# Reloading the residual on GpSimd's queue, and tying the first casts of a wide weight stage in order

## The chip, the cores and the metric

The kernel runs on one core of a Trainium2 chip. Its time is the device time of one execution in microseconds. The kernel before took 2210.05 us, the median of 3 runs (2208.66 to 2213.14).

The engines of the core are named as the profile names them: PE (TensorE, matrix products; PEld is its weight load), DVE (VectorE), ACT (ScalarE), POOL (GpSimd) and SP (SyncE). Each takes its own instructions strictly in order. SP does no arithmetic here: its list is a list of DMAs, and where one of them has to wait for a semaphore, all that stand behind it wait too. POOL can issue DMAs as well.

## The reference

One layer of a transformer-like encoder on 256 tokens of width 2048, all in float32: a SwiGLU feed-forward block (FFN1), a mixer of attention and a linear recurrence, a cross-attention, and a second feed-forward block (FFN2). The change touches only the second half of the two feed-forward blocks: the product with `w_down` (5504 x 2048) and what follows it.

```python
def rmsnorm(x, g, eps=EPS):
    xf = x.astype(jnp.float32)
    y = xf * lax.rsqrt(jnp.mean(xf * xf, axis=-1, keepdims=True) + eps)
    return (y * g.astype(jnp.float32)).astype(x.dtype)

def swiglu(h, w_gate, w_up, w_down):
    return (jax.nn.silu(h @ w_gate) * (h @ w_up)) @ w_down
...
h = rmsnorm(x, n_ffn1_pre[l])
x = x + 0.5 * rmsnorm(swiglu(h, w_ffn1_gate[l], w_ffn1_up[l], w_ffn1_down[l]), n_ffn1_post[l])
```

FFN2 is the same with its own weights. The `x` that is added at the end is the residual: in FFN1 the kernel's input (`in_x` in the profile), in FFN2 a copy in HBM (`xsp`).

## The kernel before

**Numbers in two parts.** A float32 product is made of three products in a faster format (float32r). Each weight tile that a DMA brings (`raw`, 128 x 1024, 512 KB) is cast on ACT to a high part (`hi`), and DVE subtracts that from the raw tile to get the low part (`lo`). PE then does high x high, high x low and low x high. So each tile needs one cast on ACT and one split on DVE before PE can use it, and its raw buffer comes free when the split is done.

**The down projection.** `ffn` first makes the hidden activations (`mh`, `ml`, 43 blocks k of 128 rows). Then `lin` runs over c = 0 to 3, the four groups of 512 output columns, two groups (b = 0: c 0 and 1, b = 1: c 2 and 3) at a time:

- For even c, the **wide part** (`lin_wide`) takes k = 0 to 29 with tiles of 1024 columns, which serve both groups. Its order is 0, 1, 2, the pair (4, 5), 3, 18, the pair (6, 7), 19, 20 and so on to the pair (16, 17) and 29. A single k costs PE 12 products: 2 token halves x 2 column halves x 3. A pair is multiplied in a Strassen-like way: its two raw tiles, here called ra and rb, are cut four times, w11 (the first half of ra), then rb as it is (w21 and w22), then, after four additions on DVE that overwrite them (L566 to L569), ra again (e1 and e3) and rb again (e4 and e2). PE uses them in the order w11, w21, w22, e1, e3, e2, e4, three products each, 21 in all. `cut` (L527) issues the cast and the split; the six slots of hi and lo that they fill go round: three are `whi`/`wlo` slots, which the other products use as well, and three are called `room`. The sums of activations that pairs need stand in `S`; those of the first five pairs lie in the buffer with the tag `big`.
- Then a **narrow part** takes k = 30 to 42 with tiles of 512 columns, two k per tile: first k = 30 to 35 of the odd group (`narrow(c + 1, ...)`), then 30 to 42 of the even one, and, in the next call of `lin`, the rest of the odd one. That is 36 + 78 + 42 = 156 products of 512 columns on PE for each b. The work of `fix_wide`, which adds the shared sums of the wide part to the results, stands between them on DVE.

**Loads.** Weight tiles go round four buffers `wraw`, and in the wide part also the two halves of `raws` (the 5th and 6th of each six loads). All are issued from SP, so a load waits on SP until the split that frees its buffer is done, and what stands behind it waits as well.

**The residual X.** `X` takes the buffer `big` again, so it can be loaded when the first five pairs of b = 1 are done. `refill` (L875) issues its four pieces (two token halves t, two column halves, 512 KB each) in the narrow part of c = 2 from SP's queue, each tied with `after` behind the last split that was written before it. `refill(k)` is called for k = 30, 33, 36 and 39, and the loop that calls it passes each k twice (once for each t): eight loads. The second of each two writes the same bytes as the first, and waits for it.

**What sets the order.** PE's order is written out by hand in these parts. On ACT, DVE, SP and POOL a scheduler places instructions by priority (`ahead` raises it) and by its own estimate of when they are ready; ties made by `after` bind it. The fixed order on each engine is the result.

Of the kernel before, what the change touches and what calls it, by code (L numbers as in the profile page):

```python
# [10 lines left out]
F32 = mybir.dt.float32  # L11
# [7 lines left out]
P = 128  # L19
D = 2048  # L20
T = 256
NT = T // P
# [14 lines left out]
SPAIRS = range(2, 9)  # L37
WIDE, EARLY = 30, 36


def _wide_order():

    rest = [k for k in range(WIDE) if k // 2 not in SPAIRS]
    out, rest = rest[:3], rest[3:]
    for i in SPAIRS:
        out.append((2 * i, 2 * i + 1))
        out, rest = out + rest[:2], rest[2:]
    assert not rest
    return out
# [176 lines left out]
class Layer:  # L226
# [288 lines left out]
        self.split(d[:, 0], mh[:, k, P:], ml[:, k, P:])  # L515
        self.split(d[:, 1:], sh, sl)

    def lin_wide(self, w, b, mh, ml, sums, ring, raws, banks):

        nc = self.nc
        own, shared = banks
        seen, turn = set(), [0]
        last = _wide_order()[-1]

        def cut(raw):  # L527
            n = raw.shape[-1]
            hi, lo = (x[:, :n] for x in ring[turn[0] % len(ring)])
            turn[0] += 1  # L530
            with self.ahead(self.lead):
                self.last_cast = nc.scalar.copy(out=hi, in_=raw)  # L532
                self.last_split = nc.vector.tensor_sub(out=lo, in0=raw, in1=hi.bitcast(F32))  # L533
            return [(self.paired(hi[:, i : i + 512]), self.paired(lo[:, i : i + 512])) for i in range(0, n, 512)]

        def product(bank, x, wt, stop=False):
            (xh, xl), (hi, lo) = x, wt
            start = id(bank) not in seen
            seen.add(id(bank))
            nc.tensor.matmul(bank, xh, hi, start=start, stop=False)  # L540
            nc.tensor.matmul(bank, xh, lo, start=False, stop=False)  # L541
            nc.tensor.matmul(bank, xl, hi, start=False, stop=stop)  # L542

        def load():
            i = self.wide_at % 6
            raw = raws[:, i - 4] if i > 3 else self.wraw.tile([P, WT], F32, tag="wraw", name="wraw")
            o = P * WT * (b * KF + self.wide_at)
            nc.sync.dma_start(out=raw, in_=w[o : o + P * WT].rearrange("(p x) -> p x", p=P))
            self.wide_at += 1
            return raw  # L550

        at = lambda k, t: tuple(x[:, k, t * P : (t + 1) * P] for x in (mh, ml))
        self.wide_at = 0
        for item in _wide_order():
            if isinstance(item, int):
                halves = cut(load())
                for t in range(NT):
                    for h in range(2):
                        product(own[t][h], at(item, t), halves[h], item == last)
                continue  # L560
            k0, k1 = item
            ra, rb = load(), load()
            a0, a1, b0, b1 = ra[:, :512], ra[:, 512:], rb[:, :512], rb[:, 512:]
            (w11,), (w21, w22) = cut(a0), cut(rb)
            with self.ahead(self.lead):
                nc.vector.tensor_add(a0, a0, a1)  # L566
                nc.vector.tensor_add(a1, a1, b1)  # L567
                nc.vector.tensor_add(b1, a0, b1)
                nc.vector.tensor_add(b0, b1, b0)  # L569
            (e1, e3), (e4, e2) = cut(ra), cut(rb)  # L570
            s2, s3, s4 = sums(k0 // 2 - SPAIRS[0])
            end = k0 // 2 == SPAIRS[-1]
            product(shared[0], at(k0, 0), w11, end)
            product(own[0][0], at(k1, 0), w21)
            product(own[0][1], s4, w22)
            product(shared[1], at(k0, 1), e1, end)
            product(shared[2], s3, e3, end)
            product(shared[3], s2, e2, end)
            product(own[1][0], at(k1, 1), e4)
        self.cuts = turn[0]  # L580

    def fix_wide(self, banks, part):
# [210 lines left out]
    def ffn(self, normed, wg, wu, wd, post, residual, *after):  # L793
        nc = self.nc
        passage = normed if isinstance(normed, Passage) else None
        h, row, *feed = (passage.h, passage.row) if passage else normed
        with self.tc.tile_pool(name="hid", bufs=1) as hid:
            mh = hid.tile([P, KF, T], F32R, tag="mh", name="mh")
            ml = hid.tile([P, KF, T], F32R, tag="ml", name="ml")
# [3 lines left out]
            def sums(n):  # L803
                x, n = (S[0], n) if n < 5 else (S[1], n - 5)
                return x[:, 3 * n : 3 * n + 3]
# [24 lines left out]
            for c0 in range(0, DFF, 256):  # L830
                n = min(256, DFF - c0)
# [38 lines left out]
            raws = self.hpool.tile([P, 2, WT], F32, tag="hT", name="raws", bufs=4)  # L870
            slots = [(self.whi[:, a : a + WT], self.wlo[:, a : a + WT]) for a in range(0, RING * SLOT, SLOT)]
            more = [(x[:, 0], x[:, 1]) for x in room]
            fresh = {}

            def refill(k):  # L875
                i = (k - WIDE) // 3
                if "X" in fresh and i < 4:
                    t, s = i // 2, slice(i % 2 * 1024, (i % 2 + 1) * 1024)
                    self.after(nc.sync.dma_start(
                        out=fresh["X"][:, t, s], in_=residual[t * P : (t + 1) * P, s]), self.last_split)  # L880

            banks = {}

            def narrow(c, ks, ev, *args):
                base = c // 2 * KF * P * WT + (WIDE * WT + c % 2 * (KF - WIDE) * 512) * P
                for k in self.lin_tok_steps(
                        wd, KF, 0, 512, mh, ml, ev, *args, 0, [banks[c // 2][0][t][c % 2] for t in range(NT)],
                        (ks, lambda k: base + (k - WIDE) * P * 512)):
                    if c == 2 and k % 3 == WIDE % 3:
                        refill(k)  # L890

            def lin(c, ev, passage):
                b = c // 2
                if c % 2:
                    narrow(c, range(EARLY, KF, 2), ev, (7 if passage else SKEW) * (c == 3), passage)
                    return
                make = lambda pool, tag: [pool.tile([P, 512], F32, tag=tag, name="mm") for _ in range(2)]
                one = [make(self.pst, "tr"), make(self.pss, "sm")]
                two = [make(self.psm, "mm"), make(self.psm, "mm")]
                own, shared = (two, one) if b else (one, two)  # L900
                banks[b] = [list(x) for x in zip(*own)], [x for p in shared for x in p]
                with self.tc.manual_schedule(engines={mybir.EngineType.PE}):
                    order = slots[self.turn :] + slots[: self.turn]
                    self.lin_wide(wd, b, mh, ml, lambda n: [(x[:, 0], x[:, 1]) for x in (sums(n)[:, i] for i in range(3))],
                                  order + more, raws, banks[b])
                    self.turn = (self.turn + self.cuts % (2 * RING)) % RING if self.cuts % (2 * RING) < RING else self.turn
                    narrow(c + 1, range(WIDE, EARLY, 2), None, 0, None)
                    self.fix_wide(banks[b], self.wraw.tile([P, WT], F32, tag="wraw", name="part"))
                    if b:
                        self.X = fresh["X"] = self.hpool.tile([P, NT, D], F32, tag="big", bufs=1, name="X")  # L910
                    narrow(c, range(WIDE, KF, 2), ev, 0, None)

            return self.post_norm(lin, post, True, *after)

    def rope_tables(self, tp):
# [1022 lines left out]
```

## Time and profile before

| | |
|---|---|
| median of 3 runs | 2210.05 us |
| the profiled execution | 2216.57 us |
| span of its trace | 2214.7 us |
| granted PE clock over the span | 0.996 |
| FFN1, wide part of b = 0 / narrow / wide part of b = 1 / narrow | begins at 460.8 / 537.9 / 571.5 / 644.7 us |
| FFN2, the same | begins at 1980.0 / 2053.6 / 2087.3 / 2160.4 us |
| DMAs X<-in_x and X<-xsp in the two narrow parts | 8 and 8, 512 KB each |

Times in the trace count from the span's start. "Busy" of PE is the modelled duration of its pipelined products, which overlap: how far PE is from its pace is read from the starts and the number of its products. A row of the timeline gives the start, the duration, the engine, the line, the operation with its output and inputs, and in brackets the idle time of the engine before it with what ended that. A wait in the list of waits is followed by the total in us, the number of times and the longest.

### The profile page before, as it was taken

The page shows a single profiled execution, that of the slowest core. Times are in us where ns is not written, and L with a number is a line of the kernel's source. Part 1 is how long each engine was busy: PE and PEld are TensorE (multiplying, and loading weights), DVE is VectorE, ACT ScalarE, POOL GpSimd, SP SyncE. Part 2 cuts the span into 40 slices and gives each one's busy share as a digit, 9 for nine tenths or more (in the row PEclk, how much of TensorE's full clock was granted, in tenths as well). Part 3 has the DMA queues.
Part 4 walks back from the last instruction along what each step waited for, and adds up shares of the span by engine and source line. Part 5 has one row for each costly group of instructions (what it writes and reads, how often), then busy time and mean ns, then how long its engine had stood idle before and what let it go on. Part 6 is the DMA issues. An engine that isn't in the chain of part 4 may idle for free.

```text
span 2214.7 us, 35352 instructions
## 1 busy us (share of the span) xinstructions
PE 2170.6 (98%) x13580; PEld 1929.0 (87%) x13580; DVE 1618.7 (73%) x2402; ACT 1189.7 (54%) x1794; POOL 106.0 (5%) x177
## 2 busy tenths in 40 slices
PE   9999999999998999999999999999999999999997
PEld 8999999988887888988777889988999999988885
DVE  7777666688876677777787767657777766679795
ACT  7555555555545665664444556446555555555452
POOL 0000000000000100101342000000000000000000
PEclk9999999999999999999999999999999999999999
DMA  7666666665757664555867765546666666666755
GB/s 248 201 199 203 202 202 201 200 228 196 227 196 260 201 224 142 187 176 181 250 196 241 269 219 191 177 165 219 200 199 202 201 201 202 202 215 220 222 200 199
DMA packets 133512, 457.70 MB, mean 207 GB/s; under 512 B 16480, under 2 KB 18016, under 8 KB 133088
## 3 DMA queue, kind: packets, MB, share of 16 engines
q1 hardware_dynamic: 125712, 438.23, 60.4%
q0 software_dynamic: 6768, 16.79, 2.5%
q8 instruction: 106, 1.74, 0.3%
q10 hardware_dynamic: 864, 0.44, 0.1%
q14 instruction: 62, 0.51, 0.1%
HBM read 442.80 MB, written 12.59 MB: 206 GB/s over the span
## 4 chain that ended last, share of the span: by engine, by line
PE 80%; issue 7%; DMA 4%; DVE 4%; ACT 2%; POOL 1%; SPq 0%; DVEq 0%; POOLq 0%; ACTq 0%
PE mm L421 31%; PE mm L425 15%; PE mm L460 6%; PE mm L461 6%; PE mm L462 6%; PE mm L541 4%; PE mm L542 4%; PE mm L540 4%; DVE wlo L366 2%; ACT whi L365 1%; DMA wraw<-in_w_ffn_down 1%; DMA raws<-in_w_ffn_down 1%; DMA X<-xsp 0%; DMA X<-in_x 0%; DMA ab<-vsh 0%
## 5 line engine op out<-in xcount | busy, mean ns | idle before, releaser
L366 DVE TENSOR_TENSOR wlo<-wraw,whi 128x1024 fp32r<-128x1024 f32 (+3 forms) x672 | 806.4, 1203 | 434.9 <-ACT whi L365 426.4
L421 PE MATMUL mm<-hT,whi 128*128 128x512 f32 x3280 | 1078.2, 384 | 2.6 <-ACT whi L365 2.0
L365 ACT CAST whi<-wraw 128x1024 fp32r<-128x1024 f32 (+3 forms) x672 | 691.4, 1031 | 594.9 <-PE mm L462 209.0
L425 PE MATMUL mm<-hT,wlo 128*128 128x256 f32 x3280 | 879.7, 273 | 0.0
L421 PEld LDWEIGHTS mm<-hT,whi 128*128 128x128 f32 x3280 | 614.1, 190 | 83.7 <-ACT whi L365 3.2
L425 PEld LDWEIGHTS mm<-hT,wlo 128*128 128x128 f32 x3280 | 629.6, 192 | 6.1 <-DVE wlo L366 0.5
L461 PE MATMUL mm<-wlo,hT 128*128 128x512 f32 (+2 forms) x512 | 180.3, 352 | 3.7 <-DVE wlo L366 3.5
L460 PE MATMUL mm<-whi,hT 128*128 128x512 f32 (+2 forms) x512 | 182.5, 356 | 0.9 <-DVE gt L1597 0.7
L462 PE MATMUL mm<-whi,hT 128*128 128x512 f32 (+2 forms) x512 | 178.3, 349 | 0.3 <-DVE hT L649 0.3
L433 ACT COPY half<-mm 128x256 f32<-128x256 f32 x206 | 75.7, 368 | 115.7 <-PE mm L421 115.7
L434 DVE TENSOR_TENSOR half<-half,mm 128x256 f32<-128x256 f32 x206 | 85.9, 418 | 40.3 <-ACT half L433 40.3
L461 PEld LDWEIGHTS mm<-wlo,hT 128*128 128x128 f32 x512 | 97.1, 190 | 18.7 <-DVE wlo L366 10.1
L541 PE MATMUL mm<-wlo,mh 128*128 128x512 f32 x284 | 108.4, 382 | 1.1 <-DVE wlo L533 1.0
L540 PE MATMUL mm<-whi,mh 128*128 128x512 f32 x284 | 108.5, 382 | 0.7 <-ACT whi L532 0.7
L542 PE MATMUL mm<-whi,ml 128*128 128x512 f32 x284 | 108.4, 382 | 0.0
L460 PEld LDWEIGHTS mm<-whi,hT 128*128 128x128 f32 x512 | 97.1, 190 | 12.5 <-DVE gt L1597 1.1
L462 PEld LDWEIGHTS mm<-whi,hT 128*128 128x128 f32 x512 | 97.1, 190 | 9.9 <-DVE hT L649 1.2
L613 POOL TENSOR_TENSOR rstd<-rstd,mhalf 128x1 f32<-128x1 f32 x22 | 15.3, 704 | 1707.5 <-DVE rstd L611 1707.5
L461 PE MATMUL mm<-wlo,mh 128*128 128x512 f32 x200 | 78.2, 391 | 6.5 <-DVE wlo L366 6.5
L532 ACT CAST room<-wraw 128x1024 fp32r<-128x1024 f32 (+1 forms) x56 | 49.7, 893 | 63.3 <-DVE wraw L567 53.2
L460 PE MATMUL mm<-whi,mh 128*128 128x512 f32 x200 | 77.5, 388 | 5.1 <-ACT whi L365 5.1
L533 DVE TENSOR_TENSOR wlo<-wraw,whi 128x1024 fp32r<-128x1024 f32 x60 | 71.8, 1222 | 14.5 <-ACT whi L532 13.7
(371 smaller groups left out, 2834.6 us busy)
## 6 DMA issues: line engine op xcount, KB each, us to landing
wraw<-in_w_ffn_up SPq DMA_DIRECT2D x171, 512.0 KB, 4.2
wraw<-in_w_ffn_gate SPq DMA_DIRECT2D x170, 512.0 KB, 4.3
wraw<-in_w_ffn_down SPq DMA_DIRECT2D x128, 512.0 KB, 4.8
wraw<-in_w_in SPq DMA_DIRECT2D x124, 512.0 KB, 4.1
raws<-in_w_ffn_down SPq DMA_DIRECT2D x40, 512.0 KB, 4.8
wraw<-in_w_o SPq DMA_DIRECT2D x32, 512.0 KB, 4.2
wraw<-in_w_ckv SPq DMA_DIRECT2D x32, 512.0 KB, 3.5
wraw<-in_w_oa SPq DMA_DIRECT2D x16, 512.0 KB, 3.5
```

Of the source, the lines that this page charges most:

```text
L365: cast = self.last_cast = nc.scalar.copy(out=hi[:, e], in_=raw[:, e])
L366: self.last_split = nc.vector.tensor_sub(out=lo[:, e], in0=raw[:, e], in1=hi[:, e].bitcast(F32))
L421: both = lambda: nc.tensor.matmul(ps[j], hi[:, s], self.woven(x[:, k]), start=(k == 0), stop=(k == nk - 1))
L425: nc.tensor.matmul(ps[j][:, 0, :], lo[:, s], self.woven(x[:, k, 0]), start=False, stop=False)
L433: nc.scalar.copy(out=tokens, in_=low)
L434: nc.vector.tensor_add(tokens, tokens, high)
L460: nc.tensor.matmul(ps[t], part(xh, t, k), hi, start=(k == first and not begun), stop=False, **more)
L461: nc.tensor.matmul(ps[t], part(xh, t, k), lo, start=False, stop=False, **more)
L462: self.last_mm = nc.tensor.matmul(ps[t], part(xl, t, k), hi, start=False, stop=(k == last), **more)
L540: nc.tensor.matmul(bank, xh, hi, start=start, stop=False)
L541: nc.tensor.matmul(bank, xh, lo, start=False, stop=False)
L542: nc.tensor.matmul(bank, xl, hi, start=False, stop=stop)
```

## The change

It does two things.

**X moves.** The four loads of X are issued from POOL's queue and no longer from SP's, and once each: they are popped from a list. X's tile is made before the wide part of b = 1. `lin_wide` calls `done` behind each pair; behind the last two pairs, (14, 15) and (16, 17), that issues pieces 0 and 1. Pieces 2 and 3 are issued in the narrow part at k = 30. Each is tied behind the last split written before it.

**Ties.** In each wide part the first five calls of `cut` (those of k = 0, 1, 2, w11 and the first rb) are tied: cast behind the cast before it, split behind the split before it.

```diff
@@ lin_wide @@
+            before = self.last_cast, self.last_split
             with self.ahead(self.lead):
                 self.last_cast = nc.scalar.copy(out=hi, in_=raw)
                 self.last_split = nc.vector.tensor_sub(out=lo, in0=raw, in1=hi.bitcast(F32))
+            if turn[0] < 6:
+                for ins, prev in zip((self.last_cast, self.last_split), before):
+                    self.after(ins, prev)
...
             product(own[1][0], at(k1, 1), e4)
+            done(k0 // 2 - SPAIRS[0])
@@ ffn @@
-            fresh = {}
-
-            def refill(k):
-                i = (k - WIDE) // 3
-                if "X" in fresh and i < 4:
-                    t, s = i // 2, slice(i % 2 * 1024, (i % 2 + 1) * 1024)
-                    self.after(nc.sync.dma_start(
-                        out=fresh["X"][:, t, s], in_=residual[t * P : (t + 1) * P, s]), self.last_split)
+            fresh = []
+
+            def refill():
+                i = fresh.pop()
+                t, s = i // 2, slice(i % 2 * 1024, (i % 2 + 1) * 1024)
+                self.after(nc.gpsimd.dma_start(
+                    out=self.X[:, t, s], in_=residual[t * P : (t + 1) * P, s]), self.last_split)
...
-                    if c == 2 and k % 3 == WIDE % 3:
-                        refill(k)
+                    if fresh and k % 5 == WIDE % 5:
+                        refill()
...
+                    if b:
+                        self.X = self.hpool.tile([P, NT, D], F32, tag="big", bufs=1, name="X")
+                        fresh.extend((3, 2, 1, 0))
                     order = slots[self.turn :] + slots[: self.turn]
...
-                                  order + more, raws, banks[b])
+                                  order + more, raws, banks[b], lambda n: n > 4 and fresh and refill())
...
-                    if b:
-                        self.X = fresh["X"] = self.hpool.tile([P, NT, D], F32, tag="big", bufs=1, name="X")
```

The first place is the narrow part of b = 1 in FFN1. On SP before, the loads of X stand between those of the weights (L357):

```order
L357 DMA wraw<-in_w_ffn_down 128x1024 x6
L879 DMA X<-in_x 128x1024 x2
L357 DMA wraw<-in_w_ffn_down 128x1024
L879 DMA X<-in_x 128x1024 x2
L357 DMA wraw<-in_w_ffn_down 128x1024
L879 DMA X<-in_x 128x1024
L357 DMA wraw<-in_w_ffn_down 128x1024
L357 DMA wraw<-in_w_ffn_down 128x512
L879 DMA X<-in_x 128x1024 x2
L357 DMA wraw<-in_w_ffn_down 128x1024 x2
L879 DMA X<-in_x 128x1024
L357 DMA wraw<-in_w_ffn_down 128x1024
```

In the change SP has only weights there (9 tiles, a half one, 3 tiles, a half one), and POOL has the four loads of X, between the powers that make the norms' factors:

```order
L618 TENSOR_TENSOR rstd<-rstd,mhalf 128x1 x2
L883 DMA X<-in_x 128x1024 x4
L618 TENSOR_TENSOR rstd<-rstd,mhalf 128x1
L996 MEMSET krT 128x512
L618 TENSOR_TENSOR rstd<-rstd,mhalf 128x1 x7
```

So eight loads leave SP and four come to POOL, which has nothing else to do at that time. FFN2 is alike.

The second place is the start of the wide part of b = 0 in FFN1. The raw tiles there are wraw_4377, 4393 and 4409 (k = 0, 1, 2), wraw_4425 (ra of the pair (4, 5)), raws_4362 (both halves of it: rb of that pair, and k = 3) and wraw_4476 (k = 18). sg, half, mh and ml belong to the last block of the projection before. ACT before:

```order
L532 CAST whi_112<-wraw_4393 128x1024
L532 CAST room_4359<-wraw_4425 128x512
L813 ACTIVATE sg_4308<-sg_4308 128x256
L532 CAST room_4360<-raws_4362 128x1024
L532 CAST whi_112<-wraw_4409 128x1024
L433 COPY half_4353<-mm_4312 128x256
L532 CAST room_4361<-wraw_4425 128x1024
L646 CAST mh_125<-sg_4308 128x256
L532 CAST whi_112<-raws_4362 128x1024 x2
```

ACT in the change:

```order
L533 CAST whi_112<-wraw_4393 128x1024
L818 ACTIVATE sg_4308<-sg_4308 128x256
L533 CAST whi_112<-wraw_4409 128x1024
L533 CAST room_4359<-wraw_4425 128x512
L533 CAST room_4360<-raws_4362 128x1024
L433 COPY half_4353<-mm_4312 128x256
L533 CAST whi_112<-raws_4362 128x1024
L533 CAST room_4361<-wraw_4425 128x1024
L651 CAST mh_125<-sg_4308 128x256
L533 CAST whi_112<-wraw_4476 128x1024
L533 CAST whi_112<-raws_4362 128x1024
```

The cast of k = 2 moves ahead of those of w11 and rb. Behind them the order moves too: k = 3 (the first whi<-raws) comes ahead of e1 and e3 (room_4361), and e4 and e2 (the second whi<-raws) come behind k = 18.

DVE at the same place, before:

```order
L533 TENSOR_TENSOR room_4359<-wraw_4425,room_4359 128x512
L814 TENSOR_TENSOR sg_4308<-sg_4308,row_459 128x256
L566 TENSOR_TENSOR wraw_4425<-wraw_4425 128x512
L533 TENSOR_TENSOR room_4360<-raws_4362,room_4360 128x1024
L533 TENSOR_TENSOR wlo_114<-wraw_4409,whi_112 128x1024
L567 TENSOR_TENSOR wraw_4425<-wraw_4425,raws_4362 128x512
L434 TENSOR_TENSOR half_4353<-half_4353,mm_4312 128x256
L568 TENSOR_TENSOR raws_4362<-wraw_4425,raws_4362 128x512
L819 TENSOR_TENSOR sg_4308<-half_4353,sg_4308 128x256
L569 TENSOR_TENSOR raws_4362<-raws_4362 128x512
L533 TENSOR_TENSOR room_4361<-wraw_4425,room_4361 128x1024
L533 TENSOR_TENSOR wlo_114<-raws_4362,whi_112 128x1024 x2
```

DVE in the change, from the split of rb on; those of k = 2 and w11 stand just ahead of it:

```order
L534 TENSOR_TENSOR room_4360<-raws_4362,room_4360 128x1024
L570 TENSOR_TENSOR wraw_4425<-wraw_4425 128x512
L434 TENSOR_TENSOR half_4353<-half_4353,mm_4312 128x256
L571 TENSOR_TENSOR wraw_4425<-wraw_4425,raws_4362 128x512
L824 TENSOR_TENSOR sg_4308<-half_4353,sg_4308 128x256
L572 TENSOR_TENSOR raws_4362<-wraw_4425,raws_4362 128x512
L534 TENSOR_TENSOR wlo_114<-raws_4362,whi_112 128x1024
L573 TENSOR_TENSOR raws_4362<-raws_4362 128x512
L534 TENSOR_TENSOR room_4361<-wraw_4425,room_4361 128x1024
L651 TENSOR_TENSOR ml_126<-sg_4308,mh_125 128x256
L534 TENSOR_TENSOR wlo_114<-wraw_4476,whi_112 128x1024
L534 TENSOR_TENSOR wlo_114<-raws_4362,whi_112 128x1024
```

The split of k = 2 has left the stretch between rb and e1/e3, that of k = 3 has come into it, and that of k = 18 now stands between e1/e3 and e4/e2. The start of FFN2's first wide part has the same rows. At the start of both second wide parts (b = 1) the same order holds behind rb; there the cast and split of rb stood, in the kernel before, at the end of the first wide part (535 us in FFN1), and now stand behind those of k = 0, 1, 2 and w11. On SP the loads change places by one or two at these starts.

More of the change, by code (lines that the diff above doesn't have):

```diff
@@ L516, in left, with lin_wide @@
         self.split(d[:, 1:], sh, sl)
-    def lin_wide(self, w, b, mh, ml, sums, ring, raws, banks):
+    def lin_wide(self, w, b, mh, ml, sums, ring, raws, banks, done):
         nc = self.nc
```

## The prediction

> **What bounds the kernel now.** I read the page first, for the engine that sets the end:
>
> ```profile
> span 2214.7 us, 35352 instructions
> ...
> PE 80%; issue 7%; DMA 4%; DVE 4%; ACT 2%; POOL 1%; SPq 0%; DVEq 0%; POOLq 0%; ACTq 0%
> ```
>
> PE carries 80% of the chain that ended last, DMA 4%. PE sets the pace, so a change can gain only where PE pauses. To find pauses I asked for the windows of the narrow parts: the first row is that of b = 0 in FFN1, with no load of X, the others are those of b = 1 in FFN1 (up to its first transposes) and in FFN2. The columns are length, busy time and number of instructions of each engine, then clock, DMA share and GB/s.
>
> ```profile
> 537.86:571.46 33.60, 33.60 (x157) 29.44 (x156) 20.80 (x23) 15.25 (x19) 0.00 (x0) 1.00 0.67 212
> 644.64:688.15 43.51, 35.93 (x147) 28.27 (x146) 22.61 (x30) 15.63 (x21) 0.55 (x1) 0.96 0.75 260
> 2160.42:2204.07 43.65, 37.66 (x157) 29.95 (x155) 21.57 (x29) 13.73 (x19) 0.55 (x1) 0.96 0.60 205
> ```
>
> The first is the measure of this forecast: the same 156 products (157 with one that reaches over the edge) took 33.60 us, 0.2154 us each, without a pause. In FFN1's second narrow part 147 products should take 31.7 us and took 43.5: **11.8 us lost**. In FFN2's 156 should take 33.6 and took 43.65: **10.0 us lost**. The losses hold some product time at a lower clock (0.96). Then I read the chain of waits there (start, duration, what):
>
> ```profile
> 663.01 5.64 DMA X<-in_x
> 668.67 0.33 SPq L879
> 669.10 4.95 DMA X<-in_x
> 674.07 0.33 SPq L879
> 674.49 7.06 DMA wraw<-in_w_ffn_down
> ...
> 2178.48 6.17 DMA X<-xsp
> 2185.10 4.63 DMA X<-xsp
> 2190.17 7.05 DMA wraw<-in_w_ffn_down
> ```
>
> PE waits for a weight tile, its load waits for SP's issue of X (L879), and that for an earlier load of X. The waits of SP's queue give the whole (total, times, longest):
>
> ```profile
> SPq L879 <- DVE wlo L366: 15.8, 6, 4.2
> ...
> SPq L879 <- DMA X<-xsp: 13.1, 4, 4.9
> SPq L879 <- DMA X<-in_x: 13.0, 4, 4.3
> ```
>
> For 41.9 us SP stood at a load of X: behind the split it is tied to, or, for a second load of one piece, behind the first load. Each time the next weights are issued too late.
>
> The second place with pauses is the start of FFN1's first wide part. PE's rows there, k = 2 first, w11 last:
>
> ```profile
> 465.74 0.38 PE L542 MATMUL mm<-whi,ml 128*128 128x512 f32 x1
> 466.81 0.48 PE L540 MATMUL mm<-whi,mh 128*128 128x512 f32 x1 [0.69 <-ACT whi L532]
> 468.26 0.51 PE L541 MATMUL mm<-wlo,mh 128*128 128x512 f32 x1 [0.96 <-DVE wlo L533]
> ...
> 472.42 0.38 PE L540 MATMUL mm<-room,mh 128*128 128x512 f32 x1
> ```
>
> From 465.74, 13 products at 0.2154 would put w11 at 468.54; it came at 472.42: **3.9 us lost**, part of it by a clock of 0.57 behind the gaps:
>
> ```profile
> 468.00:472.00 4.00, 3.74 (x10) 3.00 (x11) 4.00 (x8) 2.94 (x4) 0.00 (x0) 0.57 0.44 135
> ```
>
> ACT shows why:
>
> ```profile
> 464.76 1.04 ACT L532 CAST room<-raws 128x1024 fp32r<-128x1024 f32 x1 [1.82 <-DMA raws<-in_w_ffn_down]
> 465.71 1.04 ACT L532 CAST whi<-wraw 128x1024 fp32r<-128x1024 f32 x1
> ```
>
> The cast of k = 2 stands behind that of rb, which waits for its load. In FFN2 the same place loses 0.4 us: 12 products from 1985.15 would put w11 at 1987.74.
>
> ```profile
> 1985.15 0.38 PE L540 MATMUL mm<-whi,mh 128*128 128x512 f32 x1
> ...
> 1988.15 0.38 PE L540 MATMUL mm<-room,mh 128*128 128x512 f32 x1
> ```
>
> The second wide parts begin without a gap.
>
> **Part 1: X leaves SP.** Eight issues and the waits in front of them go from SP's queue in each narrow part. What remains is the queue of b = 0, and that ran 156 products in 33.60 us. So I take all that was lost: 11.8 + 10.0 = **21.8 us gained**. What is late next is PE itself. The last 10.6 us, from PE's last product in FFN2 (2204.07) to the end of the span, are not touched.
>
> The cost of the move is 4 issues on POOL, before no row of that stage. The nearest rows, eight loads in the mixer and a stretch there in which DVE was busy 31.56 of 36 us:
>
> ```profile
> L1733 POOL DMA_DIRECT2D t<-t1d x8: 536/538/604, 1170.3 to 1215.3; - x8
> ...
> 1168.00:1204.00 36.00, 33.46 (x155) 27.62 (x154) 31.56 (x43) 15.08 (x18) 11.76 (x14) 1.00 0.77 252
> ```
>
> So 4 x 0.54 = 2.2 us on an engine that was busy 0.55 us in all of the stage. On POOL the norm's powers stand behind them, and those need the end of the block anyway. Pieces 0 and 1 are tied to the splits of the last two pairs, 2 and 3 to that of k = 30, whose row, with that of the updates of X (the first at 687.7), is:
>
> ```profile
> 638.87 1.22 DVE L366 TENSOR_TENSOR wlo<-wraw,whi 128x1024 fp32r<-128x1024 f32 x1 [0.42 <-ACT whi L365]
> ...
> L764 DVE SCALAR_TENSOR_TENSOR X<-y,rstd,X x31: 742/746/1755, 687.7 to 2208.1; 128x512 f32<-128x512 f32 x31
> ```
>
> From 640.1 to 687.7 less 11.8 gained is 36 us of cover for landings of 5 to 6 us (those in the chain above). Were it gone, each block would lose one landing. `big` is free by then: the five pairs that read it come earlier in PE's order.
>
> Their bytes still use the 16 DMA engines: 4 x 512 KB = 2.1 MB, at the 409 GB/s that FFN2's start reached
>
> ```profile
> 1980.00:1985.00 5.00, 5.00 (x25) 4.38 (x24) 3.37 (x5) 3.20 (x5) 0.00 (x0) 1.00 1.01 409
> ```
>
> is 5.1 us. The weights need 212 GB/s, and up to four tiles of 2.6 us of PE's time each (12 products) are ahead. So the cost lies between 0 and 5.1 us in each block; I take 0, by the first window, whose DMA share of 0.67 leaves a third free.
>
> **Part 2: the ties.** Their gain is the cast of k = 2; their cost is the new order behind it. DVE's pace comes from FFN2's start:
>
> ```profile
> 1983.26 1.23 DVE L533 TENSOR_TENSOR room<-raws,room 128x1024 fp32r<-128x1024 f32 x1
> 1984.40 1.22 DVE L533 TENSOR_TENSOR wlo<-wraw,whi 128x1024 fp32r<-128x1024 f32 x1
> 1985.54 0.68 DVE L567 TENSOR_TENSOR wraw<-wraw,raws 128x512 f32<-128x512 f32 x1
> 1986.14 0.41 DVE L434 TENSOR_TENSOR half<-half,mm 128x256 f32<-128x256 f32 x1
> 1986.47 0.68 DVE L568 TENSOR_TENSOR raws<-wraw,raws 128x512 f32<-128x512 f32 x1
> ```
>
> Start to start a split of 1024 takes 1.14 us, an addition of 512 columns 0.60, one of 256 columns 0.33. In the new order, from rb's split to the end of e4/e2's: four of 1.14 (rb, k 3, e1/e3, k 18), four of 0.60, three of 0.33 and a last 1.23 make 9.18 us. FFN2: 1983.26 + 9.18 = 1992.44. PE, now without a gap, asks for the low part of e2 after 28 products from 1985.15 (12 of k = 2, 15 of the pair, one high): at 1991.18. It waits 1.26 us; 0.41 goes away: **0.85 us lost**. FFN1: rb's cast came when its load did, so its split starts at 464.76 + 1.04, about 465.8. e1/e3 is then split 6.57 later, at 472.4 (the list up to it, with 1.23 for itself), and PE asks for it at 465.95 + 22 x 0.2154 = 470.7; e4/e2 comes at 475.0 and is asked for, 28 products and that wait behind 465.95, at 473.7. The waits are 1.7 + 1.3 = 3.0 us, with no clock loss, or 4.7 if the clock falls again (4.0 us at 0.57 are 1.7 lost), against 3.9: I take **0**, nearest to the middle. In the b = 1 parts rb's cast and split are new work at the start. There PE begins k = 0 at:
>
> ```profile
> 571.49 0.38 PE L540 MATMUL mm<-whi,mh 128*128 128x512 f32 x1
> ...
> 571.47 1.23 DVE L533 TENSOR_TENSOR wlo<-wraw,whi 128x1024 fp32r<-128x1024 f32 x1 [1.36 <-ACT whi L532]
> ...
> 573.45 0.59 ACT L640 ACTIVATE junk<-mm 128x512 f32<-128x512 f32 x1
> ```
>
> DVE, from the split of k = 1 at 571.47: 1.14, then an output's product 0.60, k = 2 at about 573.4 (on ACT its cast, 1.04, now follows a square like the row above, and both wait for PE's last product ahead of 571.49), then 1.14, w11 0.60, rb 1.14, an addition, a second output's product and two additions (2.40), k 3 1.14, an addition 0.60, e1/e3 1.14, k 18 1.14 and 1.23: 583.9. PE asks for e2's low part after 52 products, at 582.7: **1.2 us lost**, twice. Sum of the ties: 0 + 0.85 + 2.4 = **3.3 us lost**. From both sides: at best k = 2's 3.9 and 0.4 come back and no new wait shows (4.3 gained); at worst each new wait trips the clock as in FFN1, 1.7 each: 0.8 + 2.55 + 2.9 + 2.9 = 9.2 lost.
>
> **The sum** against the profiled execution (2216.57 us: its span and 1.9 around it): 2216.57 - 21.8 + 3.3 = 2198.1. That execution lies 6.5 us above the median of the runs. The same 18.5 off the median, 2210.05, is 2191.6; I say **2192 us**.
>
> **Rivals.**
> 1. *The ties cost nothing*: DVE's and ACT's true waits differ from my list, and k = 2's gain stays. 2210.05 - 21.8 - 4.3 = 2184. For it: the second wide parts had no gap. Against: the rows of the order.
> 2. *Every new wait trips the clock*: 2210.05 - 21.8 + 9.2 = 2197.5. For it: 0.57 at 468 us. Against: FFN1's narrow part lost 11.8 us in gaps and kept 0.96 on the mean.
> 3. *X, or the weights beside it, land late.* Either X crowds the weights out of the DMA engines, 5.1 us a block, or POOL's issues stand until DVE rests at the end of the part, and each block waits for one landing, 5.6: up to 2191.6 + 11.2 = 2202.8. For it: the DMA share of 1.01 where loads bunch. Against: the share of 0.67, and the mixer's issues, 604 ns at the longest beside a DVE that was busy 88%. The Trainium skill, "SBUF — State Buffer", section "SBUF: two separate sides", has a rule for the second case: certain VectorE instructions hold a shared port, and GpSimd cannot write the descriptors of its DMAs meanwhile. The trace does not agree for the instructions that ran in the mixer, hence a small share of this rival's chance.
> 4. *The queue makes no difference*: only SP's time of issuing is saved, 8 x 0.33 us a block,
>
> ```profile
> L879 SPq DMA_DIRECT2D X<-in_x x8: 328/328/378, 651.8 to 674.1; - x8
> ```
>
> 5.3 in all: 2210.05 - 5.3 + 3.3 = 2208. Against it: the 41.9 us in which SP stood. The Trainium skill, "DMA: Bandwidth & Descriptors", section "Issuing engines are not separate DMA queues", says just this, that issuing from several engines saves only the sequencer's issue time; here what SP loses is waiting, which that sentence leaves out.
> 5. *Slower*: k = 3's split now stands ahead of e1/e3's, so if its load or its cast comes late, DVE stands, and in this stage it has nothing to make that up with: behind FFN2's start it was busy 9.85 of 10 us.
>
> ```profile
> 1990.00:2000.00 10.00, 10.00 (x48) 8.63 (x47) 9.85 (x13) 5.69 (x7) 0.00 (x0) 1.00 0.66 218
> ```
>
> At 6 us for each of the four starts: 24 + 3.3 - 21.8 = 5.5, 2215.6. It decides from 4.6 us a start. Among the listed waits of ACT none is of a cast into whi of this line behind a load.
>
> **How the numbers follow.** The forecast 0.67 (2188 to 2196), rival 1 0.10, rival 2 0.10, rival 3 0.08, rival 4 0.03, rival 5 0.02. The range reaches from rival 1 to rival 3, 2184 to 2203, and leaves out rivals 4 and 5. A measurement of this kernel tells some 0.2% (4.4 us) from no change: faster by more than that 0.95, within it 0.03 (rival 4), slower 0.02.
>
> **What would show it.** Right: no X in SP's waits, 156 products in about 33.6 us in FFN2's last narrow part, DMA gone from the chain there, and waits of 1 to 2 us at e1 or e2 in four wide parts. Wrong: narrow parts that still take over 36 us, X landing after 670 us, or wide parts that begin without a gap or with gaps over 3 us.

## The result, and the profile after

The changed kernel takes **2195.38 us** (median of 4 runs, 2194.65 to 2195.59); the kernel before took 2210.7 us beside it (4 runs, 2208.66 to 2213.14). The ratio is 0.993, with a 95% interval from 0.9912 to 0.9947: 15.3 us faster. The forecast was 2192.0 us, in a range from 2184 to 2203. The profiled execution took 2195.21 us, 21.4 us less than the profiled one of before.

The page after, its span and its chain of waits:

```profile
span 2193.4 us, 35347 instructions
...
PE 45%; DVE 5%; issue 1%; DMA 1%; ACT 1%; POOL 0%; DVEq 0%; POOLq 0%; ACTq 0%
```

The shares of this chain add up to 53%: it could not be followed back to the start, and FFN1 is not in it. DMA is down from 4% to 1%, but the windows say more. Those of the stages that the change touches, after (length, busy time and number of instructions of PE, PEld, DVE, ACT and POOL, then clock, DMA share, GB/s); each begins with PE's first product of its part and ends with the first of the next one, in FFN1's last narrow part with the first transpose. In order: FFN1's wide part of b = 0, of b = 1, its narrow part of b = 1, and the same of FFN2.

```profile
459.83:534.33 74.50, 73.46 (x340) 63.91 (x339) 67.01 (x76) 42.04 (x46) 0.00 (x0) 1.00 0.65 227
568.00:642.45 74.45, 73.70 (x340) 63.91 (x339) 68.18 (x75) 42.49 (x48) 2.34 (x4) 1.00 0.67 221
642.45:674.27 31.82, 31.82 (x148) 27.59 (x146) 22.92 (x31) 16.05 (x21) 0.56 (x1) 1.00 0.76 250
1965.57:2040.51 74.94, 73.70 (x340) 63.91 (x339) 66.99 (x76) 42.34 (x46) 0.00 (x0) 1.00 0.65 226
2074.18:2148.64 74.46, 73.71 (x341) 63.91 (x339) 68.20 (x75) 42.50 (x48) 2.16 (x4) 1.00 0.66 220
2148.64:2182.09 33.45, 33.45 (x156) 29.30 (x155) 21.13 (x29) 13.83 (x19) 0.56 (x1) 1.00 0.49 162
```

The two narrow parts run without a pause (busy time equals length, clock 1.00) and take 31.82 + 33.45 = **65.27 us**. The four wide parts have 339 products each, 73.0 us at 0.2154; they take 74.50 + 74.45 + 74.94 + 74.46 = **298.35 us**, 6.3 over their pace. Their pauses are where the ties are. PE and DVE at the start of FFN1's second wide part (timelines):

```profile
579.32 0.38 PE L544 MATMUL mm<-whi,S 128*128 128x512 f32 x1
580.40 0.48 PE L545 MATMUL mm<-wlo,S 128*128 128x512 f32 x1 [0.71 <-DVE wlo L534]
```

```profile
576.86 1.22 DVE L534 TENSOR_TENSOR room<-wraw,room 128x1024 fp32r<-128x1024 f32 x1
578.00 1.22 DVE L534 TENSOR_TENSOR wlo<-wraw,whi 128x1024 fp32r<-128x1024 f32 x1
579.13 1.22 DVE L534 TENSOR_TENSOR wlo<-raws,whi 128x1024 fp32r<-128x1024 f32 x1
```

These DVE rows are the splits of e1/e3, of k = 18 and of e4/e2; that of k = 3 went ahead of them at 575.12. PE asks for e2's low part at 579.53 (one product of 0.2154 behind the high one) and gets it at 580.40. The loads of X stand on POOL (timeline):

```profile
625.71 0.72 POOL L883 DMA_DIRECT2D X<-in_x  x1 [585.67 <-DVE wlo L534]
635.42 0.54 POOL L883 DMA_DIRECT2D X<-in_x  x1 [8.99 <-DVE wlo L534]
638.18 1.07 POOL L883 DMA_DIRECT2D X<-in_x  x2 [2.22 <-DVE wlo L366]
```

### The profile page after: what moved, and what is told of

Same layout as the page of the kernel before. It is cut to its first block, busy times and chain, and to the rows that moved or that the text cites. A ratio compares the mean times of both kernels' runs of the same rounds, so it can differ in the third digit from the quotient of the medians.

```text
span 2193.4 us, 35347 instructions
## 1 busy us (share of the span) xinstructions
PE 2161.4 (99%) x13580; PEld 1926.9 (88%) x13580; DVE 1617.8 (74%) x2402; ACT 1190.3 (54%) x1794; POOL 110.5 (5%) x185
## 4 chain that ended last, share of the span: by engine, by line
PE 45%; DVE 5%; issue 1%; DMA 1%; ACT 1%; POOL 0%; DVEq 0%; POOLq 0%; ACTq 0%
PE mm L421 16%; PE mm L425 8%; PE mm L460 5%; PE mm L462 4%; PE mm L461 4%; PE mm L545 2%; PE mm L546 2%; PE mm L544 2%; DVE wlo L366 2%; ACT whi L365 0%; DVE tm L1415 0%; DVE TT L1418 0%; PE xo L1817 0%; PE tr L663 0%; DMA raws<-in_w_ffn_down 0%
## 5 line engine op out<-in xcount | busy, mean ns | idle before, releaser
L533 ACT CAST whi<-wraw 128x1024 fp32r<-128x1024 f32 x60 | 61.3, 1048 | 31.6 <-ACT whi L533 9.0
```

## The experiments

One theory stood first, **A**: X's waits in SP's order are the whole gain, and the ties cost a little. Its rivals: the doubled loads, or the new places, do it and not the queue; the ties carry a part. All results in one table; "narrow over" is what the two last narrow parts take over 65.27 us, "wide" the sum of the four wide parts, both from one profiled execution by windows like those above.

| kernel | us | ratio to before, 95% | narrow over | wide |
|---|---|---|---|---|
| before, the profile of the forecast | 2216.57 | | 22.0 | 297.0 |
| before, a second profile | 2211.03 | | 20.7 | 294.6 |
| changed | 2195.38 | 0.993 (0.9912 to 0.9947) | 0 | 298.4 |
| changed, beside the others | 2194.72 | 0.9926 (0.9912 to 0.994) | 0 | 297.9 |
| X's move alone | 2191.32 | 0.9909 (0.9894 to 0.9924) | 0 | 293.6 |
| ties alone | 2215.89 | 1.0018 (1.0009 to 1.0027) | 22.8 | 298.2 |
| before, X once, on SP | 2198.56 | 0.9942 (0.9929 to 0.9954) | 7.7 | 293.9 |
| before, X twice, on POOL | 2196.18 | 0.9926 (0.9914 to 0.9939) | 5.3 | 295.2 |
| before, X once, on POOL | 2193.28 | 0.9919 (0.9905 to 0.9932) | 1.2 | 293.8 |
| changed, X on SP | 2194.16 | 0.9921 (0.9908 to 0.9935) | 0 | 297.8 |
| changed, X on SP and twice | 2203.62 | 0.9967 (0.9954 to 0.9979) | 11.0 | 299.3 |
| changed, nine cuts tied | 2189.55 | 0.99 (0.9887 to 0.9914) | 0 | 292.7 |

**1. The kernel before, a second profile.** No edit.

> The kernel before, unchanged, for a second profiled execution. Theory A (the pauses at X's loads vary from execution to execution, and the profiled one of before had long ones): this execution lies near the median of 2210 us, and the last narrow parts of FFN1 and FFN2 lose together 14 to 19 us in place of 21.8. Rival (the pauses are the same in every execution, and the 6.5 us by which the profiled one lay above the median come from elsewhere): 21.8 us again, within 1 us.

Measured: 2211.03 us, and 43.26 + 42.75 us in the narrow parts, 20.7 over. The same six windows as above:

```profile
459.61:533.32 73.71, 73.48 (x341) 63.91 (x339) 68.25 (x77) 42.98 (x48) 0.00 (x0) 1.00 0.67 230
566.99:640.16 73.17, 73.17 (x341) 64.07 (x340) 67.12 (x74) 41.47 (x47) 0.00 (x0) 1.00 0.62 206
640.16:683.42 43.26, 35.69 (x149) 28.34 (x147) 22.95 (x31) 15.94 (x21) 0.55 (x1) 0.96 0.78 261
1974.13:2048.14 74.01, 73.49 (x340) 63.91 (x339) 68.23 (x77) 43.01 (x48) 0.00 (x0) 1.00 0.67 229
2081.81:2155.55 73.74, 73.43 (x340) 63.99 (x339) 67.11 (x74) 41.30 (x47) 0.00 (x0) 1.00 0.62 205
2155.55:2198.30 42.75, 37.02 (x157) 30.03 (x155) 21.34 (x29) 13.74 (x19) 0.55 (x1) 0.96 0.61 209
```

Theory A was wrong on this point, and the rival nearer: the narrow parts lose nearly as much here (20.7 against 22.0). What differs is FFN1's first wide part, 73.71 us where the profile of the forecast has (its window)

```profile
460.77:537.82 77.05, 75.39 (x341) 65.17 (x339) 68.53 (x77) 43.70 (x48) 0.00 (x0) 0.98 0.63 221
```

and ACT shows why (timeline of the second profile):

```profile
461.90 1.05 ACT L532 CAST room<-raws 128x1024 fp32r<-128x1024 f32 x1 [0.27 <-DMA raws<-in_w_ffn_down]
462.85 1.05 ACT L532 CAST whi<-wraw 128x1024 fp32r<-128x1024 f32 x1
```

rb's load had landed at 461.9 and not at 464.76, and the cast of k = 2 behind it was nearly in time: PE lost 0.4 us there (464.79 to 465.39 for two products in a row). The loss of 3.9 us in the forecast is therefore that execution's and not the kernel's; its 2216.57 us lie above all 37 other timed executions of before beside these runs (2208.49 to 2213.52).

**2. X's move alone.** The changed kernel, with

```diff
-            if turn[0] < 6:
+            if False:
```

> X as in the changed kernel, without the ties. Theory A (X's move is the whole gain; the ties cost 1.4 us, the difference of the four starts in the two profiles, 5.7 against 4.3): 2194 us, between 2191 and 2197; the narrow parts without a pause, FFN1's first wide part with the late cast of k = 2 again. Rival (the ties carry a part of the gain that the four starts don't show): 2200 us or more. The prediction's own price of the ties (3.3 us lost): 2192.

Measured: 2191.32 us, ratio 0.9909. A wide and a narrow part of its windows, FFN1's first wide and last narrow:

```profile
461.21:534.83 73.62, 73.48 (x340) 63.91 (x339) 68.23 (x77) 42.98 (x48) 0.00 (x0) 1.00 0.67 230
...
641.67:673.49 31.82, 31.82 (x148) 27.60 (x147) 22.79 (x31) 16.04 (x21) 0.56 (x1) 1.00 0.73 248
```

The narrow parts are as after; the wide ones need 293.6 us in place of 298.35. X's move is the whole gain, 20.8 us (from 2212.12, the median of before beside it), and the ties take some of it back: 4.1 us by time (2195.38 - 2191.32), nearer to the 3.3 of the prediction than to the 1.4 of theory A.

**3. The ties alone.** The diff of `lin_wide` without the call of `done`; X as before.

> The ties alone, X on SP's queue as before. Theory A: 2212 us, between 2208 and 2216, with pauses in the last narrow parts and X in SP's waits as before. Rival (the ties carry a part of the gain): 2205 us or less.

Measured: 2215.89 us, ratio 1.0018: 3.8 us lost, against the 1.4 that two unlike profiles had let me expect. Both experiments give the ties about the same price, and neither finds a gain of theirs.

**4. The changed kernel again, and with nine cuts tied**, on one chip.

```diff
-            if turn[0] < 6:
+            if turn[0] < 10:
```

> The changed kernel, unchanged, beside the next three on one chip. Theory B (X's move gains 20 to 22 us in every execution; the ties cost about 1.3 us at each of the four starts against an execution of before without FFN1's late cast, so some 4 us): 2195.4 us, within 1 us, each wide part between 74.4 and 75.0 us for its 339 products where the kernel with X alone needs 73.2 to 73.6.

> The changed kernel with the first nine cuts of each wide part tied in order in place of the first five, so that VectorE splits e1/e3 and then e4/e2 ahead of k = 3 and k = 18. Theory B (what the ties cost is e4/e2 behind these two splits, 2 x 1.14 us): the four pauses at e2 go, 4.5 to 5.7 us gained, 2190 us, between 2188.5 and 2192. Rival (VectorE is short of time at these starts in any order): the pauses move to k = 3 or k = 18, 2195 us.

Measured: 2194.72 and **2189.55 us**. With nine ties the splits of e1/e3 and e4/e2 stand ahead of those of k = 3 and k = 18. DVE and PE at the same place as above:

```profile
575.29 1.22 DVE L534 TENSOR_TENSOR room<-wraw,room 128x1024 fp32r<-128x1024 f32 x1
576.55 2.36 DVE L534 TENSOR_TENSOR wlo<-raws,whi 128x1024 fp32r<-128x1024 f32 x2
578.82 1.22 DVE L534 TENSOR_TENSOR wlo<-wraw,whi 128x1024 fp32r<-128x1024 f32 x1
```

```profile
578.45 0.38 PE L544 MATMUL mm<-whi,S 128*128 128x512 f32 x1
578.66 0.38 PE L545 MATMUL mm<-wlo,S 128*128 128x512 f32 x1
```

The low part of e2 comes one pace behind the high one. The four wide parts take 73.17, 73.17, 73.16 and 73.17 us: no pause is left. So DVE had the time; only its order was wrong. This kernel is 5.2 us under the changed kernel beside it, at 0.99 of before (0.9887 to 0.9914). That it beats X's move alone (0.9909, 0.9894 to 0.9924) is not shown: the intervals overlap, the two ran on different chips, and their wide parts differ by 0.9 us only (293.6 against 292.7).

> The kernel with nine cuts tied, once more for a second profile: the four wide parts 73.2 us each again and the narrow parts without a pause, some 2189.5 us.

Measured, the same kernel once more: 2188.91 us, wide parts 73.16 to 73.17 us, narrow parts 65.27.

**5. The queue, the place and the count of X's loads.** Before with each piece once, on SP at the old places:

```diff
-                if "X" in fresh and i < 4:
+                if "X" in fresh and i < 4 and i not in fresh:
+                    fresh[i] = True
```

> The kernel before, on SP at the same places, but each piece of X loaded once: the second loads and their waits behind the first ones (26.1 of the 41.9 us in SP's waits) are gone, the waits behind a split (15.8 us) stay. Theory A (every wait of X's issues in SP's order delays the next weights): part of the loss stays, in the ratio of the waits 15.8 / 41.9 of some 17 us, so 2200 us, between 2197 and 2206. Rival (the second loads and their bytes are all of it): 2194 us, no pause. Rival (only the place behind a split counts): 2208 us or more.

Measured: 2198.56 us, inside theory A's 2197 to 2206, and 7.7 over in the narrow parts. The second loads were nearly two thirds of the loss, a third stays. Its windows, and its waits of SP on X's line (there L880):

```profile
640.58:675.42 34.84, 32.66 (x148) 27.35 (x146) 22.73 (x31) 15.95 (x21) 0.55 (x1) 1.00 0.74 253
2146.80:2184.90 38.10, 35.67 (x156) 30.40 (x155) 21.15 (x29) 13.84 (x19) 0.55 (x1) 0.96 0.51 179
```

```profile
SPq L880 <- DVE wlo L366: 22.0, 8, 5.9
```

The changed kernel with its four loads on SP (`nc.gpsimd.dma_start` becomes `nc.sync.dma_start` in `refill`):

> The changed kernel with its four loads of X issued on SP's queue, at the same new places, once each. Theory A (it is the order of SP's queue: whatever waits for a split there holds the weights behind it): X is in SP's waits again, some of the loss returns, 2197 to 2205 us. Rival (the new places and the single loads suffice, the queue makes no difference): 2195.4 us, within 1.5 us.

Measured: 2194.16 us against 2194.72 for the changed kernel on the same chip. **Theory A falls here.** X is back on SP, SP waits for splits (X's line, L883),

```profile
SPq L883 <- DVE wlo L534: 15.0, 4, 6.6
SPq L883 <- DVE wlo L366: 4.8, 2, 2.4
```

and the narrow parts have no pause at all (windows):

```profile
642.61:674.42 31.81, 31.81 (x149) 27.60 (x147) 22.94 (x31) 16.07 (x21) 0.55 (x1) 1.00 0.73 240
2147.20:2180.65 33.45, 33.45 (x156) 29.30 (x155) 21.15 (x29) 13.84 (x19) 0.55 (x1) 1.00 0.46 155
```

SP's timeline in FFN1 shows how (a row can join several issues):

```profile
625.58 0.33 SPq L883 DMA_DIRECT2D X<-in_x  x1
626.00 2.69 SPq L357 DMA_DIRECT2D wraw<-in_w_ffn_down  x3
635.29 3.58 SPq L883 DMA_DIRECT2D X<-in_x  x3
638.98 11.13 SPq L357 DMA_DIRECT2D wraw<-in_w_ffn_down  x4
```

Three tiles of the narrow part are issued by 628.7, ahead of the long wait. PE begins that part at 642.61 and needs 2.6 us for each, so the fourth tile is asked for at about 650; issued at 638.98, it has 11 us.

The same on POOL at the old places, with two loads of each piece (the kernel before with `nc.gpsimd.dma_start`):

> The kernel before with its eight loads of X, at the old places and two for each piece, issued on GpSimd's queue; no ties. Theory A (only the weights behind X in SP's queue lose; the bytes and the doubled loads are hidden): 2191 us, as X alone at the new places, between 2189 and 2195. Rival (the doubled loads cost by their bytes, 2.1 MB more in each block at 409 GB/s, 5.1 us): 2196 to 2202. Rival (the last pieces land late for the update of X, each behind its first load): up to 5 us a block, 2196 to 2201.

Measured: 2196.18 us (three of five executions; the other two took 2193.34 and 2193.80), ratio 0.9926, 3.0 + 2.3 = 5.3 us over in the narrow parts: the lower end of what the rival of bytes had. The queue is the only difference to the kernel before, which took 2210.94 us beside it. FFN1's last narrow part:

```profile
641.61:676.42 34.81, 32.69 (x149) 27.43 (x147) 22.86 (x31) 15.96 (x21) 5.04 (x9) 1.00 0.84 309
```

309 GB/s and a DMA share of 0.84, the highest of all these narrow parts; in the chain there one load of weights takes 7.56 us to land (663.00 to 670.56), and PE pauses until 671.16 for the tile ahead of that one, which ACT could cast only when it had landed, at 668.8. The median load of 512 KB of weights took 6.1 us to land in this part and 7.2 in FFN2's, against 4.4 and 4.7 in the changed kernel. With that, theory **C**: what SP waits costs only what exceeds the weights already issued; the doubled loads cost some more by their bytes. That it is their bytes, and not how they wait for one another, is argued and not shown apart. Two runs for it. First, once each on POOL at the old places (both edits together):

> The kernel before with each piece of X loaded once, at the old places, on GpSimd's queue. Theory C (at the old places the weights' issues behind X in SP's order lose the time; the second loads lose some more by their bytes, as the 5.3 us that remained with doubled loads on GpSimd's queue): no pause in the last narrow parts, 65.3 us for the two together, 2191 us, between 2189 and 2194. Rival (at the old places even single loads crowd out the weights; the 7.7 us that remained with single loads on SP are of this kind): the two narrow parts 68 to 73 us, 2195 to 2199.

Measured: 2193.28 us, narrow parts 32.78 + 33.67 = 66.45 us: 1.2 over, nearer to C than to its rival. Of the 7.7 us that stay with single loads on SP, 6.5 are SP's order. Then the changed kernel on SP, with each load issued twice:

```diff
-                self.after(nc.gpsimd.dma_start(
-                    out=self.X[:, t, s], ...), self.last_split)
+                for _ in range(2):
+                    self.after(nc.sync.dma_start(
+                        out=self.X[:, t, s], ...), self.last_split)
```

> The changed kernel with its loads of X on SP's queue and each of them issued twice, at the new places. Theory C (a wait in SP's order costs what it exceeds the weights already issued ahead; single loads at the new places stay below that, the waits of second loads behind first ones don't): the last narrow parts lose 4 to 12 us again, 2198 to 2207. Rival (the new places alone do it, whatever SP waits there): 2194 us, within 1.5 us.

Measured: 2203.62 us, ratio 0.9967, 11.0 over in the narrow parts, as C had it. SP in FFN1, with the second loads behind the first ones:

```profile
627.03 1.04 SPq L357 DMA_DIRECT2D wraw<-in_w_ffn_down  x2
632.47 0.33 SPq L884 DMA_DIRECT2D X<-in_x  x1
632.89 0.38 SPq L357 DMA_DIRECT2D wraw<-in_w_ffn_down  x1
636.33 10.41 SPq L884 DMA_DIRECT2D X<-in_x  x5
646.82 0.38 SPq L357 DMA_DIRECT2D wraw<-in_w_ffn_down  x1
```

The fourth tile now leaves at 646.82, 3 us after PE began the narrow part (643.64). Three tiles last PE 36 x 0.2154 = 7.8 us, to 651.4; its last product ahead of the pause starts at 651.20. Neither the queue nor the place alone is the cause: either the single loads at the new places or the other queue is enough for most of it.

## Why the prediction was right, and where it was off

**The bound.** PE sets the pace, and the pauses were in the narrow parts: right. PE lost 22.0 us there in the profiled execution, and all of it went.

**Part 1, 21.8 us gained.** Right in size: 22.0 us against the profiled execution, 20.7 against the second one, 20.8 by time for X's move alone. The measure for it, the narrow part of b = 0, was the right one. "X leaves SP" was not needed for it, though: the prediction took the 41.9 us of waits as the cause and weighed neither the new places nor the single loads as causes. With 19.8 us of waits at the new places nothing is lost. The right size shows that no pause was left, and not that the queue was what removed it. The cost of X's bytes, taken as 0, was 0 in the kernel as changed. Its upper bound of 5.1 us in each block held even for doubled loads at the old places on POOL (3.0 and 2.3). POOL's four issues took 0.54 to 0.72 us each in FFN1, close to the 0.54 of the mixer, and nothing waited for them.

**Part 2, 3.3 us lost.** The mechanism was right: the main pauses stand at e2's low part, behind the splits of k = 3 and k = 18. For the second wide parts the list of DVE's work gave 1.2 us; they take 74.45 - 73.17 = 1.28 longer in FFN1. For FFN2's first wide part it gave 0.85; that takes 74.94 - 73.63 = 1.31 longer than in the profile of the forecast. **The term that was mis-sized is FFN1's first wide part, taken as 0**: 3.9 gained by k = 2 against new waits of 3.0 to 4.7. Against the profiled execution it gained 77.05 - 74.50 = 2.55 us; rb's load landed at 461.9 in the changed kernel's execution, where the prediction had put it at 464.76, so the new wait was short. Against a usual execution of before, where rb lands as early and k = 2 is nearly in time, it lost 74.50 - 73.71 = 0.8 us. That 0 is not far from this is luck: neither the 3.9 us gained nor a wait at e1 is there, only one of 1.2 us at e2's low part. Summed over the four, the ties cost 298.35 - 294.63 = 3.7 us in the profiles, 3.8 by time when they stand alone and 3.4 to 4.1 as the difference of the changed kernel (2194.72 and 2195.38) and X's move alone (2191.32).

**The sum.** This is the step that failed, by 3 us. The prediction worked out 18.5 us against the profiled execution and took the same off the median. Profile to profile the change gave 21.4, more than that, most of it from the late load of rb in that execution, on which the ties gained 2.55 us where 0 was taken. Median to median it gave 15.3, less. From a usual execution, the second profile, it adds up: narrow parts -20.7 (1.1 less than forecast), wide parts +3.7 (0.4 more lost), and +1.3 outside of these stages make -15.7, the difference of the spans (2193.4 - 2209.1). The prediction put the last term at nothing, and no run here explains it.

**The rivals.** That the ties cost nothing, or that every new wait trips the clock, did not happen: no clock was lost in the wide parts after. X or the weights landing late did not happen in the kernel as changed. "The queue makes no difference" was given 0.03 as a forecast of 2208 us, and that was right to refuse; but for the changed kernel it comes out: at the new places the two queues give the same time within 0.6 us. The Trainium skill's page "DMA: Bandwidth & Descriptors", section "Issuing engines are not separate DMA queues", says that issuing from several engines saves only the sequencer's issue time, and these two runs agree with it. At the old places the runs do not: doubled loads took 2210.94 on SP and 2196.18 on POOL beside it, single ones 2198.56 on SP and 2193.28 on POOL. The slower case, a late split of k = 3, did not come.

**What stays open.** Why single loads on POOL at the old places still lose 1.2 us was not tried; 0.5 of it is the wait of FFN1's first transpose for the update of X (PE's starts at 672.60 and 673.30). Doubled loads on POOL at the new places were not run. How often rb lands late in FFN1's first wide part is not known either: of the six profiles without ties, one has 77.05 us there and the others 73.6 to 74.4.

## What to carry to other kernels

A wait in an in-order list of loads costs only what it exceeds the loads already issued: count the tiles ahead of the waiting one and compare their compute time with the wait before moving anything to another queue. A loop that issues the same transfer twice makes the second wait for the first, which was the larger half of the loss here. A tie that brings one operation forward puts another one back, so tie all that the consumer's order asks for, or nothing (here the four wide parts took 292.7 us with nine ties, 293.6 with none and 298.4 with five); and before a price that one profiled execution shows once is carried over to a median, take a second profile.

## What the hardware showed beside this

PE's granted clock after a pause is not decided by the length of the pause alone. In the second profile of before, PE had its last product ahead of a gap at 655.48, one at 657.54 and the next at 658.80, and at 670.87, 673.52 and 674.78 again. The stretches behind the two (windows):

```profile
659.00:663.00 4.00, 4.00 (x11) 2.98 (x10) 0.00 (x0) 0.64 (x1) 0.00 (x0) 0.57 0.87 272
675.20:679.20 4.00, 3.05 (x13) 2.00 (x12) 3.04 (x6) 1.63 (x3) 0.00 (x0) 1.00 0.99 342
```

Behind the first, of 3.3 us, the clock is 0.57 and products come every 0.43 us; behind the second, of 3.9 us, it stays at 1.00. The pauses of 0.9 to 1.2 us at e2's low part in the wide parts after cost no clock at all. So a pause has no fixed price: 1.7 us more (4.0 us at 0.57), or nothing.
